# Two encoder layers on one core: the last layer's products over 512 tokens in one matmul, and a layer norm applied when products leave PSUM

## The chip, the cores and the metric

The kernel runs on one core of a Trainium2 chip. The metric is the device time of one launch in microseconds; the lower, the better. Times of the kernel before are from three runs; the profile is of one further execution.

## The reference

Two layers work on 512 tokens of width 1024, float32, with 16 learned meta tokens put ahead of them (528 columns in all, the meta tokens dropped at the end). In each layer one normalised input feeds one wide projection, four mixers run on parts of it, each mixer's result is projected and gated, and an MLP follows:

```python
def hybrid_layer(h, ...):
    hn = rmsnorm(h, norm_g[0])
    (gate_pre, cb, cc, cv, mq, mk, mv, mo, mi, mf, su, cq, ckv, kr) = split_cols(hn @ w_in)
    gates = jax.nn.sigmoid(gate_pre).reshape(bsz, L, N_BRANCH, D)
    ys = (short_conv_mixer(...), mlstm_mixer(...), s5_mixer(...), mla_mixer(...))
    ...
        term = gates[:, :, bi] * (ys[bi] @ w_branch[start:start + w])
    ...
    h = h + rmsnorm(merged @ w_out, norm_g[1])
    hn = rmsnorm(h, norm_g[2])
    ff = jnp.square(jax.nn.relu(hn @ w1)) @ w2
    return h + rmsnorm(ff, norm_g[3])
```

`rmsnorm` divides a token's row by the root of its mean square and multiplies by a gain per channel. Since the division is one number per token, it can be made before a product or after it.

## The kernel before, in words

Activations lie channel by channel: 128 channels on the partitions, tokens along the free axis. A product takes a weight tile of 128 x 128 as the stationary operand and streams tokens. Every float32 operand is split in a high and a low part, and a term of a product is three matmuls into one PSUM bank (`triple`, lines 473 to 477): high weight by high activation, high by low, low by high. `prod` (line 465) runs over the terms, eight for a product over 1024 channels.

The tokens stand in two halves (`HALF`, line 24): 272 columns with the meta tokens and 256. In the last layer the meta tokens are only needed as keys and values, so most products there run over `LAST` (line 25), two halves of 256. Each weight tile is therefore used for two separate accumulations of 256 columns.

Weights come from HBM in units of 512 KB; ScalarE makes the high part (`cut`), VectorE the low part (`rest`). Activations lie in 32 slots of SBUF. `Wide` keeps 528 columns of two channel tiles in one slot; `Tok` keeps a half of the tokens, four channel tiles to a slot, so that the two halves of one channel tile lie in different slots.

The order of the work is written by a planner inside the program. It follows the main line of products and keeps an estimate of the time on TensorE, VectorE and ScalarE (class `Model` and the engine wrappers). Side work (the mixers, norms, evictions) is a set of generators; `tick` gives each a turn when its operands are due and VectorE and ScalarE are at most 2.05 us ahead of TensorE by these estimates (line 501). `drain` puts TensorE off until a generator has ended, `room` until slots are free. So a change of one piece moves all that comes after it.

A layer begins with its 17 units of the input projection (`unit`, line 1567). Its operand is the layer input times the gain, not yet divided by the norm, since the norm is not known so early; `evac` (line 1516) multiplies by the norm row `R` when a product leaves PSUM. Meanwhile `rescale` (line 1615) reads the layer input a second time from HBM, scales it with gain and norm and splits it anew into `X2`; `fresh` (line 1638) puts each half in place of the first copy as soon as it is there. From then on a product leaves PSUM by a plain ScalarE copy, and a gate by ScalarE's tanh straight from PSUM (`gate`, line 1675). mLSTM waits until the state-space branch S5 and the rescaling have ended (line 1662). The branches follow (`branch`, line 1689), the attention inputs, the output projection, and the MLP in two rounds of 16 units up (`up`, `relu2`) and 16 down (`down`, line 1994). `place` reserves slots for weight tiles that must be held over both halves.

## Time and profile before

| what | value |
|---|---|
| median of three runs | 1978.32 us |
| the three runs | 1979.14, 1974.87, 1978.32 us |
| the profiled execution's own time | 1978.66 us |
| its span, first to last instruction | 1976.8 us |
| mean granted TensorE clock | 0.984 |

The span is what the profile's shares refer to; 1.9 us of the execution lie around it. A row of TensorE is a matmul, named by where it writes, what streams and what is stationary (`mm<-H,hi` streams a slot against the high part of a weight). Durations of matmuls overlap, so the pace is read from starts. The clock column is the granted clock as a share of full speed.

### The profile page before, as it was taken

What the parts mean: (1) busy time and instruction counts of PE and PEld (TensorE: products, weight loads), DVE (VectorE), ACT (ScalarE), POOL (GpSimd) and SP (SyncE); (2) the same over time, 40 slices, a digit from 0 to 9 for tenths busy, and PEclk for the clock granted to TensorE, in tenths of its full rate; (3) what the DMA queues carried; (4) which work ended last, traced back from release to release, by engine and by line L of the source; (5) the groups of instructions that cost most, each with busy time, mean ns of one, the idle gap of its engine ahead of it and who ended that gap; (6) DMA issues with size and microseconds to landing.
All of it is one profiled execution on the core that took longest, in us unless ns stands there. A gap on an engine that the chain in (4) does not pass through costs nothing.

```text
span 1976.8 us, 36671 instructions
## 1 busy us (share of the span) xinstructions
PE 1911.3 (97%) x15111; PEld 1843.4 (93%) x15111; DVE 1124.9 (57%) x2785; ACT 810.6 (41%) x1752; POOL 30.2 (2%) x64
## 2 busy tenths in 40 slices
PE   7999899999989999999999999999999999999999
PEld 6998887889989999999999998899899999999998
DVE  6977675654466774244366765666545666214534
ACT  4245543543434652244233444435344455224421
POOL 0000000100000000000000000001000000000000
PEclk9999899999989999999999999999999999999999
DMA  4332121312223233222234322133212522232231
GB/s 144 102 110 81 43 65 51 95 56 63 65 94 111 86 128 118 77 95 86 90 104 179 103 86 65 38 100 116 61 47 66 171 65 86 84 99 86 89 105 65
DMA packets 56072, 176.65 MB, mean 89 GB/s; under 512 B 6433, under 2 KB 13857, under 8 KB 55905
## 3 DMA queue, kind: packets, MB, share of 16 engines
q1 hardware_dynamic: 55904, 174.31, 27.3%
q8 instruction: 118, 1.93, 0.4%
q14 instruction: 50, 0.40, 0.1%
HBM read 165.24 MB, written 7.96 MB: 88 GB/s over the span
## 4 chain that ended last, share of the span: by engine, by line
PE 84%; DVE 8%; ACT 5%; issue 2%; DMA 1%; SPq 0%; DVEq 0%; ACTq 0%
PE mm L189 68%; PE ac L189 8%; PE mx L189 6%; DVE H L162 4%; ACT H L162 3%; PE mx L195 2%; DMA raw<-in_wall 1%; DVE tq L162 1%; DVE lo L162 1%; ACT wk L162 1%; ACT hi L162 0%; DVE acc L162 0%; DMA H<-in_wall 0%; DVE a_mx L162 0%; ACT tq L162 0%
## 5 line engine op out<-in xcount | busy, mean ns | idle before, releaser
L189 PE MATMUL mm<-H,hi 128*128 128x256 f32 (+1 forms) x7104 | 1337.2, 289 | 21.0 <-ACT hi L162 7.9
L189 PEld LDWEIGHTS mm<-H,hi 128*128 128x128 f32 x7104 | 1118.7, 192 | 34.1 <-ACT hi L162 7.9
L189 PE MATMUL mm<-H,lo 128*128 128x256 f32 (+1 forms) x3552 | 1015.7, 286 | 6.5 <-DVE lo L162 6.5
L189 PEld LDWEIGHTS mm<-H,lo 128*128 128x128 f32 x3552 | 681.6, 192 | 7.5 <-DVE lo L162 7.5
L162 DVE TENSOR_TENSOR lo<-raw,hi 128x1024 fp32r<-128x1024 f32 (+1 forms) x246 | 296.1, 1214 | 176.3 <-ACT hi L162 173.2
L162 ACT ACTIVATE hi<-raw 128x1024 fp32r<-128x1024 f32 (+1 forms) x246 | 253.8, 1046 | 108.3 <-PE mm L189 64.4
L189 PE MATMUL mm<-H,H 128*128 128x256 f32 (+1 forms) x1608 | 200.2, 285 | 2.4 <-DVE H L162 2.1
L189 PEld LDWEIGHTS mm<-H,H 128*128 128x128 f32 x1608 | 196.6, 190 | 3.7 <-DVE H L162 3.7
L189 PE MATMUL ac<-H,hi 128*128 128x256 f32 (+1 forms) x752 | 145.0, 289 | 4.2 <-DVE H L162 4.0
L162 ACT ACTIVATE gt<-mm 128x256 f32<-128x256 f32 (+1 forms) x185 | 71.4, 386 | 189.0 <-PE mm L189 181.1
L162 ACT ACTIVATE H<-mm 128x256 f32<-128x256 f32 (+5 forms) x152 | 60.1, 400 | 177.7 <-PE mm L189 175.3
L189 PEld LDWEIGHTS ac<-H,hi 128*128 128x128 f32 x752 | 118.1, 190 | 6.5 <-DVE H L162 5.9
L189 PE MATMUL mx<-H,H 128*128 128x132 f32 (+10 forms) x496 | 108.9, 357 | 11.2 <-ACT H L162 6.9
L162 DVE TENSOR_TENSOR gt<-gt 128x256 f32<-128x256 f32 (+1 forms) x110 | 47.0, 428 | 113.2 <-ACT H L162 113.1
L189 PE MATMUL ac<-H,lo 128*128 128x256 f32 (+1 forms) x376 | 106.7, 284 | 0.0
L189 PEld LDWEIGHTS mx<-H,H 128*128 128x128 f32 (+1 forms) x496 | 71.0, 192 | 30.0 <-issue 15.2
L162 ACT ACTIVATE tq<-H 128x256 f32<-128x256 f32 (+2 forms) x105 | 39.3, 407 | 115.5 <-DVE H L162 115.5
L162 DVE TENSOR_REDUCE a_mx<-mx 128x1 f32<-128x144 f32 (+5 forms) x80 | 33.3, 436 | 76.5 <-PE mx L189 75.5
L162 DVE TENSOR_TENSOR acc<-acc,tq 128x256 f32<-128x256 f32 (+1 forms) x123 | 52.6, 427 | 37.1 <-ACT tq L162 34.2
L162 ACT ACTIVATE wk<-mx,a_mx 128x512 f32<-128x512 f32 (+4 forms) x88 | 40.0, 462 | 79.6 <-DVE a_mx L162 79.6
L189 PEld LDWEIGHTS ac<-H,lo 128*128 128x128 f32 x376 | 71.5, 190 | 0.0
L162 DVE TENSOR_TENSOR H<-H,tq 128x256 f32<-128x256 f32 (+2 forms) x154 | 65.3, 424 | 4.6 <-ACT H L162 1.3
(243 smaller groups left out, 1507.2 us busy)
## 6 DMA issues: line engine op xcount, KB each, us to landing
raw<-in_wall SPq DMA_DIRECT2D x274, 512.0 KB
raw<-in_wuq SPq DMA_DIRECT2D x6, 384.0 KB
H<-in_xT SPq DMA_DIRECT2D x4, 528.0 KB
hspill<-H SPq DMA_DIRECT2D x4, 528.0 KB
H<-hspill SPq DMA_DIRECT2D x4, 528.0 KB
H<-in_wall SPq DMA_DIRECT2D x4, 512.0 KB
mats<-H SPq DMA_DIRECT2D x4, 512.0 KB
H<-mats SPq DMA_DIRECT2D x4, 512.0 KB
```

What stands on the lines that cost most here:

```text
L162: i = f(*a, **k)
L189: i = self.eng.matmul(out, lhsT=lhsT, rhs=rhs, start=start, stop=stop)
L195: i = self.eng.transpose(out, in_, identity)
```

## The change

In the last layer the two halves of most products become one product of 512 columns, a whole PSUM bank. For this the slots are allocated in pairs, one tile of SBUF for two slots: `sides` gives the slots so that the halves of a channel tile lie at the same place in the two slots of a pair, and `Tok.at` then returns one operand of two runs of 256 columns. Pairs are kept apart by the kind of data (`kinds`), so free slots are counted by `avail`. The products' evictions are cut back into halves (`cut_up`), but for the MLP's, which take 512 columns at once (`ups`).

`rescale`, `X2` and `fresh` are gone. The first, undivided copy serves for the whole layer, in both layers, and gates and attention inputs are multiplied by `R` on VectorE when they leave PSUM. mLSTM waits only for free slots. `prod` gives side work a turn after every second term of a wide product, and the last layer holds one weight tile less ahead in its first MLP round and none in its last.

```diff
-LAG2 = 7
+LAG2 = 6
...
+    def whole(n=1):
+
+        ps = [i // 2 for i in free if i % 2 == 0 and i + 1 in free]
+        ps.sort(key=lambda p: max(free.index(2 * p), free.index(2 * p + 1)))
+        return ps[:n]
+
+    def beside(kind):
+        return [i for i in free if i ^ 1 not in free and kinds[i // 2] == kind]
+
+    def avail(kind="f"):
+
+        return 2 * len(whole(NSLOT)) + len(beside(kind))
...
+    def sides():
+
+        p, q = whole(2)
+        return [2 * p, 2 * q, 2 * p + 1, 2 * q + 1]
...
         def at(self, m, c0, c1):
+            if c0 < CUT < c1:
+                o, p = m % 4 * CUT + c0, self.hs[m // 4].pair
+                return p.rearrange("p (a n) -> p a n", n=SLOT)[:, :, o:o + CUT - c0]
             i = c0 // CUT
-            return self.t[2 * i + m // 4][:, m % 4, c0 - HALF[i][0]:c1 - HALF[i][0]]
+            o = 0 if i == 0 else META if self.ids else 0
+            return self.t[2 * i + m // 4][:, m % 4, c0 - HALF[i][0] + o:c1 - HALF[i][0] + o]
...
             if i % 4 == 3:
                 ahead(deep[0])
+            if i % 4 == 3 or i % 2 and ps.shape[1] > CUT:
                 tick()
...
-        X2 = Tok(0), Tok(0)
-        scaled_ = []
-
-        def rescale():
-            for c, (c0, c1) in enumerate(HALF):
-                hs = []
-                while not s5_on or len(free) < 4:
-                    yield "w"
-                for x in X2:
-                    x.more()
-                for m in range(11):
-                    if m < 8:
-                        hs.append(wk_t()[:, :c1 - c0])
-                        dma(hs[-1], (hspill if l else xT)[:, m, c0:c1])
-                    if 1 < m < 10:
-                        t = hs[m - 2]
-                        while PE.t < model.due(t):
-                            yield "w"
-                        stt(t, t, gain(l, 0, m - 2), R[:, c0:c1], ALU.mult, ALU.mult)
-                        copy(r(X2[0].at(m - 2, c0, c1)), t)
-                    if m > 2:
-                        tt(r(X2[1].at(m - 3, c0, c1)), hs[m - 3], X2[0].at(m - 3, c0, c1), ALU.subtract)
-                        yield 0
-                yield
-                scaled_.append(c)
-
-        def fresh():
-
-            for c in scaled_[len(swapped):]:
-                for x, x2 in zip((XH, XL), X2):
-                    x.drop(c)
-                    x.hs[2 * c:2 * c + 2], x.t[2 * c:2 * c + 2] = x2.hs[2 * c:2 * c + 2], x2.t[2 * c:2 * c + 2]
-                swapped.append(c)
...
-                fresh()
                 unit(w, first[j], c)
...
-                e_ml = spawn(mlstm(l, last, made["qk"], made["v"], made["o"], ym, lambda: e_s5 not in gens and e_rs not in gens))
+                e_ml = spawn(mlstm(l, last, made["qk"], made["v"], made["o"], ym, lambda: True))
...
+        WIDE = ((META, T),) if last else HALF
+
+        def cut_up(c0, c1):
+
+            return [(i, max(a, c0) - c0, min(b, c1) - c0) for i, (a, b) in enumerate(QH) if a < c1 and b > c0]
+
         def gate(w, dst_of):
-            for i, (c0, c1) in enumerate(QH):
+            for c0, c1 in WIDE:
                 ps = bank()[:, :c1 - c0]
-                fresh()
                 prod(ps, terms(w, 0, 8, xh, xl, c0, c1))
-                g = dst_of(i)
-                if i in swapped:
-                    act(g, ps, AF.Tanh, scale=0.5)
-                else:
-                    tt(g, ps, R[:, c0:c1], ALU.mult)
+                for i, a, b in cut_up(c0, c1):
+                    g = dst_of(i)
+                    tt(g, ps[:, a:b], R[:, QH[i][0]:QH[i][1]], ALU.mult)
                     act(g, g, AF.Tanh, scale=0.5)
                 lent[0] = 0
                 tick()
...
-                for i, (c0, c1) in enumerate(QH):
+                for c0, c1 in WIDE:
                     ps = bank()[:, :c1 - c0]
                     prod(ps, terms(w, (m % per) * nk * 128, nk, hi, lo, c0, c1))
-                    d = mg.at(m, c0, c1)
-                    if b == 0:
-                        stt(d, gt[i], 1.0, ps, ALU.add, ALU.mult)
-                    else:
-                        t = tq()[:, :c1 - c0]
-                        stt(t, gt[i], 1.0, ps, ALU.add, ALU.mult)
-                        tt(d, d, t, ALU.add)
+                    for i, a, e in cut_up(c0, c1):
+                        d = mg.at(m, *QH[i])
+                        if b == 0:
+                            stt(d, gt[i], 1.0, ps[:, a:e], ALU.add, ALU.mult)
+                        else:
+                            t = tq()[:, :e - a]
+                            stt(t, gt[i], 1.0, ps[:, a:e], ALU.add, ALU.mult)
+                            tt(d, d, t, ALU.add)
...
-        drain(e_rs)
-        fresh()
...
-        for i, halves in ((3, HALF), (4, HALF), (0, QH), (1, QH), (2, QH)):
+        for i, cols in ((3, HALF), (4, HALF), (0, WIDE), (1, WIDE), (2, WIDE)):
             w = W(l, U_IN + 17 + i)
-            for c0, c1 in halves:
+            for c0, c1 in cols:
                 ps = bank()[:, :c1 - c0]
-                fresh()
                 prod(ps, terms(w, 0, 8, xh, xl, c0, c1))
-                copy(rawq.at(i, c0, c1) if i < 3 else rawk.at(i - 3, c0, c1), ps)
+                for j, (h0, h1) in enumerate(HALF if i > 2 else QH):
+                    a, e = max(h0, c0), min(h1, c1)
+                    if a < e:
+                        d = rawq.at(i, a, e) if i < 3 else rawk.at(i - 3, a, e)
+                        tt(d, ps[:, a - c0:e - c0], R[:, a:e], ALU.mult)
...
+        def ups(m, w):
+            if not last:
+                for c in range(2):
+                    up(m, c, w)
+                return
+            ps = mm_t()
+            prod(ps, terms(w, 0, 8, xh, xl, META, T))
+            hh, hl = hid[m % 16 // 8]
+            t = wk_t()[:, :T - META]
+            t3 = t.rearrange("p (a n) -> p a n", a=2)
+            act(t, ps, AF.Relu)
+            hi = hh.at(m % 8, META, T)
+            act(r(hi), t3, AF.Square)
+            tt(t, t, t, ALU.mult)
+            tt(r(hl.at(m % 8, META, T)), t3, hi, ALU.subtract)
...
-        def down(d, m, c, w, first=True, fin=True, ps=None):
-            c0, c1 = QH[c]
-            n = c1 - c0
-            ps = ps if ps is not None else mm_t()[:, :n]
+        def down(d, m, cs_, w):
+
+            c0, c1 = QH[cs_[0]][0], QH[cs_[-1]][1]
+            ps = mm_t()[:, :c1 - c0]
...
+        ALL = [(0, 1)] if last else [(0,), (1,)]
...
-        lagh = place([(l, U_W2 + 16 + u) for u in range(12, 16)])
+        lagh = [] if last else place([(l, U_W2 + 16 + u) for u in range(12, 16)])
```

The order of the instructions moves with it, in three places.

TensorE, last layer, first MLP round, where one weight tile's turn ends and the next begins. Before (a bank `mm` holds 256 columns; the same weight `_19324` then comes a second time for the other half):

```order
L189 MATMUL mm_19539<-H5_18222,hi_19324 128x256
L189 MATMUL mm_19539<-H19_18224,hi_19324 128x256
L189 MATMUL mm_19539<-H5_18222,lo_19325 128x256
L189 MATMUL mm_19575<-H13_18524,hi_19324 128x256
L189 MATMUL mm_19575<-H23_18526,hi_19324 128x256
L189 MATMUL mm_19575<-H13_18524,lo_19325 128x256
```

Now:

```order
L192 MATMUL mm_17561<-H8_16441,H6_17056 128x512
L192 MATMUL mm_17561<-H15_16439,H6_17056 128x512
L192 MATMUL mx_17597<-ones_94,acc_17506 128x1 x2
L192 MATMUL mm_17621<-H0_16438,hi_17496 128x512
L192 MATMUL mm_17621<-H4_16440,hi_17496 128x512
L192 MATMUL mm_17621<-H0_16438,lo_17497 128x512
```

Each weight tile now has one accumulation of 512 columns, and the next bank begins with the next weight tile.

TensorE, layer 0: mLSTM's first transposes (`m_lf`), with S5's matmuls of 132 columns and gate products around them. Before, they stand between gate products, behind all of S5:

```order
L189 MATMUL mm_2687<-H27_1849,hi_2429 128x256
L189 MATMUL mm_2687<-H9_1851,hi_2429 128x256
L189 MATMUL mm_2687<-H27_1849,lo_2430 128x256
L195 MATMUL mx_2718<-cs_92,m_lf_2216 4x16
L195 MATMUL mx_2718<-cs_92,m_lf_2216 4x128 x2
L195 MATMUL mx_2723<-cs_92,m_lf_2216 4x128 x2
L189 MATMUL mm_2741<-H18_985,hi_2556 128x272
```

Now:

```order
L192 MATMUL mx_2060<-H15_958,H2_960 128x132
L192 MATMUL mx_2060<-H8_961,H2_960 128x132 x2
L198 MATMUL mx_2077<-cs_92,m_lf_1765 4x16
L198 MATMUL mx_2077<-cs_92,m_lf_1765 4x128 x2
L198 MATMUL mx_2082<-cs_92,m_lf_1765 4x128 x2
L192 MATMUL mx_2089<-H15_958,H2_960 128x132
```

They have moved into the output products of S5's first group, ahead of its whole second group.

VectorE, layer 0, a gate and its branch product (`tq`, then the sum in a slot) beside attention's softmax steps. Before:

```order
L162 TENSOR_SCALAR H_4243<-wk,a_sm 128x16
L162 TENSOR_SCALAR wk<-wk,a_sm 128x256
L162 TENSOR_TENSOR lo<-raw,hi 128x1024
L162 SCALAR_TENSOR_TENSOR tq<-gt,mm 128x272
L162 TENSOR_TENSOR H_1865<-H_1865,tq 128x272
L162 SCALAR_TENSOR_TENSOR tq<-gt,mm 128x256
L162 TENSOR_TENSOR H_1865<-H_1865,tq 128x256
L162 TENSOR_REDUCE a_mx<-mx 128x1 x2
```

Now:

```order
L162 TENSOR_SCALAR H_354<-wk,a_sm 128x16
L162 TENSOR_SCALAR wk<-wk,a_sm 128x256
L162 TENSOR_TENSOR gt<-mm,R 128x272
L162 TENSOR_TENSOR gt<-mm,R 128x256
L162 SCALAR_TENSOR_TENSOR tq<-gt,mm 128x272
L162 TENSOR_TENSOR H_189<-H_189,tq 128x272
L162 SCALAR_TENSOR_TENSOR tq<-gt,mm 128x256
L162 TENSOR_TENSOR H_189<-H_189,tq 128x256
L162 TENSOR_TENSOR lo<-raw,hi 128x1024
L162 TENSOR_REDUCE a_mx<-mx 128x1 x2
```

Each gate now adds two multiplications by `R` on VectorE, ahead of its branch product.

## Rows read from the trace of the kernel before

**Rows 1.** The page: span, busy times (us, share, instructions), granted clock in 40 slices.

```profile
span 1976.8 us, 36671 instructions
...
PE 1911.3 (97%) x15111; PEld 1843.4 (93%) x15111; DVE 1124.9 (57%) x2785; ACT 810.6 (41%) x1752; POOL 30.2 (2%) x64
...
PEclk9999899999989999999999999999999999999999
```

**Rows 2.** The page: the chain that ended last, shares of the span by engine.

```profile
PE 84%; DVE 8%; ACT 5%; issue 2%; DMA 1%; SPq 0%; DVEq 0%; ACTq 0%
```

**Rows 3.** Busy time by stretches, instructions behind each engine; columns in the first line.

```profile
core 0: us, PE busy (x) PEld busy (x) DVE busy (x) ACT busy (x) POOL busy (x), PEclk, DMA share, GB/s
140.00:240.00 100.00, 88.81 (x675) 86.20 (x675) 69.74 (x170) 56.00 (x124) 1.78 (x9) 0.93 0.23 72
200.00:220.00 20.00, 16.35 (x112) 16.34 (x112) 16.73 (x38) 9.11 (x21) 0.00 (x0) 0.83 0.18 54
540.00:560.00 20.00, 15.21 (x101) 11.74 (x100) 8.59 (x33) 8.71 (x29) 0.00 (x0) 0.77 0.00 0
1120.00:1140.00 20.00, 18.04 (x137) 17.88 (x137) 14.61 (x38) 8.52 (x19) 0.00 (x0) 0.91 0.39 124
1140.00:1160.00 20.00, 16.57 (x141) 16.17 (x139) 9.86 (x24) 11.89 (x26) 0.00 (x0) 0.96 0.09 27
1160.00:1180.00 20.00, 19.63 (x146) 19.63 (x147) 16.83 (x51) 6.39 (x13) 1.14 (x4) 0.87 0.42 129
1800.00:1900.00 100.00, 100.00 (x842) 100.00 (x841) 47.90 (x79) 40.34 (x75) 0.00 (x0) 1.00 0.29 90
```

**Rows 4.** Order of time on TensorE, last layer's MLP: start us, duration us, operation.

```profile
1710.04 0.40 PE L189 MATMUL mm<-H,hi 128*128 128x256 f32 x2
...
1715.76 0.40 PE L189 MATMUL mm<-H,hi 128*128 128x256 f32 x2
```

**Rows 5.** The same for the last layer's value projection, 512 columns.

```profile
1350.22 0.40 PE L189 MATMUL mm<-lo,H 128*128 128x512 f32 x1
...
1355.08 0.40 PE L189 MATMUL mm<-lo,H 128*128 128x512 f32 x1
```

**Rows 6.** VectorE by form: out<-in, shapes, count, busy us, mean ns, idle before.

```profile
L162 DVE TENSOR_TENSOR lo<-raw,hi 128x1024 fp32r<-128x1024 f32 x240 | 290.4, 1221 | 164.2 <-ACT hi L162 161.1
...
L162 DVE TENSOR_TENSOR gt<-gt 128x256 f32<-128x256 f32 x83 | 35.2, 424 | 97.9 <-ACT H L162 97.8
...
L162 DVE TENSOR_TENSOR H<-wk,H 128x256 fp32r<-128x256 f32 x29 | 12.2, 422 | 16.0 <-ACT H L162 15.7
...
L162 DVE TENSOR_TENSOR H<-mm,R 128x256 f32<-128x256 f32 x21 | 8.8, 420 | 10.1 <-PE mm L189 8.5 <-ACT R L162 1.7
...
L162 DVE SCALAR_TENSOR_TENSOR wk<-wk,pr,R 128x272 f32<-128x272 f32 x16 | 7.9, 495 | 0.4 <-DMA wk<-hspill 0.4
...
L162 DVE TENSOR_TENSOR H<-ac,H 128x512 fp32r<-128x512 f32 x8 | 5.5, 691 | 16.7 <-ACT H L162 16.7
```

**Rows 7.** ScalarE by form, the first copy of a weight tile.

```profile
L162 ACT ACTIVATE hi<-raw 128x1024 fp32r<-128x1024 f32 x240 | 248.7, 1052 | 108.3 <-PE mm L189 64.4 <-DMA raw<-in_wall 42.2 <-PE mx L189 1.5
```

**Rows 8.** Order of time on TensorE, three waits: in brackets idle us and releaser.

```profile
203.66 2.18 PE L189 MATMUL mx<-H,H 128*128 128x132 f32 x8 [3.65 <-ACT H L162]
...
359.43 0.44 PE L195 MATMUL mx<-cs,tq 128*128 128x128 f32 x2 [2.44 <-DVE tq L162]
...
1160.37 0.58 PE L189 MATMUL mm<-H,lo 128*128 128x256 f32 x1 [3.80 <-DVE lo L162]
```

**Rows 9.** Order of time before 1160 us: a VectorE row, then ScalarE.

```profile
1158.14 0.71 DVE L162 TENSOR_TENSOR H<-H,H 128x528 fp32r<-128x528 f32 x1 [3.73 <-ACT H L162]
...
1150.08 3.31 ACT L162 ACTIVATE H<-mx 32x132 f32<-32x132 f32 x8 [2.34 <-PE mx L189]
1153.42 0.43 ACT L162 ACTIVATE H<-wk 128x272 fp32r<-128x272 f32 x1
1153.87 3.25 ACT L162 ACTIVATE H<-mx 32x132 f32<-32x132 f32 x8
```

More of the change, by code (lines that the diff above doesn't have):

```diff
@@ L186, in matmul @@
         n = max(128, math.prod(rhs.shape[1:]))
+        if len(rhs.shape) == 3:
+            out = out.rearrange("p (a n) -> p a n", a=rhs.shape[1])
         cost = self.price(4 * n if rhs.dtype == F32 else n, lhsT.shape[0])
-        self.model.issue(self, cost, out, (lhsT, rhs), 0.21, start)
+        parts = [rhs] if len(rhs.shape) < 3 else [rhs[:, j] for j in range(rhs.shape[1])]
+        self.model.issue(self, cost, out, (lhsT, *parts), 0.21, start)
         i = self.eng.matmul(out, lhsT=lhsT, rhs=rhs, start=start, stop=stop)
@@ L296, in trunk, with __init__, more @@
     class Wide:
-        def __init__(self, n=8):
-            self.hs, self.t = [], []
-            for _ in range(-(-n // 2)):
+        def __init__(self, n=8, kind="f"):
+            self.hs, self.t, self.kind = [], [], kind
+            k = -(-n // 2)
+            for _ in range(k // 2):
+                for s in two(kind):
+                    self.more(s)
+            if k % 2:
                 self.more()
-        def more(self):
-            self.hs.append(Slot())
+        def more(self, slot=None):
+            self.hs.append(slot or Slot(self.kind))
             self.t.append(self.hs[-1].v(0, 2, T))
@@ L524, in tick, with room @@
                 return
-    def room(n):
+    def room(n, kind="f"):
         spins = 0
-        while len(free) < n:
+        while avail(kind) < n:
             spins += 1
@@ L808, in mlstm @@
         yield
-        while not ready() or len(free) < 5:
+        while not ready() or avail() < 5:
             yield "w"
@@ L870, in tail @@
             nqt, nq, qi0 = max(1, n // 128), min(128, n), TS.index(q0)
-            while len(free) < 1:
+            while avail() < 1:
                 yield "w"
@@ L1153, in s5_ahead @@
     def s5_ahead(l):
-        while len(free) < 4:
+        while avail() < 4:
             yield "w"
@@ L1176, in s5_group @@
         p0 = gp * 4
-        while len(free) < (5 if gp else 6):
+        while avail() < (5 if gp else 6):
             yield "w"
@@ L1258, in s5 @@
             yield from s5_params()
-        while len(free) < 10:
+        while avail() < 10:
             yield "w"
@@ L1276, in s5 @@
         release(hu, *ht)
-        while len(free) < 2:
+        while avail("r") < 2:
             yield "w"
-        y5[0] = Wide(2), Wide(2)
+        y5[0] = Wide(2, "r"), Wide(2, "r")
         for m in range(2):
@@ L1288, in lora_norm @@
     def lora_norm(l, raw, nk, box, gcol, inv, halves, ready):
-        while not ready() or len(free) < nk:
+        while not ready() or avail("r") < nk:
             yield "w"
-        box.append(Wide(2 * nk))
+        box.append(Wide(2 * nk, "r"))
         y = box[0]
@@ L1417, in mla_attn @@
             if st is not None:
-                while heads() <= st[0] or (len(yq[0]) <= st[0] // 2 and len(free) < 2):
+                while heads() <= st[0] or (len(yq[0]) <= st[0] // 2 and avail("r") < 2):
                     yield "w"
@@ L1920, in up @@
             (evac or relu2)(m, c, ps)
+            tick()
+        def ups(m, w):
+            if not last:
+                for c in range(2):
[11 more added lines that the diff above has]
+            tt(r(hl.at(m % 8, META, T)), t3, hi, ALU.subtract)
             tick()
@@ L2004, in down @@
                 tt(a, ps, a, ALU.add)
-                if last and c and m == 7:
-                    act(accs[2], a, AF.Square)
-                else:
-                    sumsq(accs[c], a, m == 0)
+                for c in cs_:
+                    a = FF.at(m, *QH[c])
+                    if last and c and m == 7:
+                        act(accs[2], a, AF.Square)
+                    else:
+                        sumsq(accs[c], a, m == 0)
             tick()
+        ALL = [(0, 1)] if last else [(0,), (1,)]
         for m in range(8):
@@ L2027, in trunk @@
             ws.append([W(l, U_W2 + 16 + m * 2 + kg) for kg in range(2)])
-            down(1, m, 0, ws[m])
-            if m < 6:
-                down(1, m, 1, ws[m])
+            for cs_ in ALL if m < 6 else [(0,)]:
+                down(1, m, cs_, ws[m])
         for hh in hid:
@@ L2062, in trunk @@
                 slack[0] = SLACK0
-            down(1, m, 1, ws[m])
+            down(1, m, (1,), ws[m])
         for hh in hid:
```

108 lines of the change are left out of this document (61 added, 47 removed).

## The prediction, made before the changed kernel ran

> **What bounds the kernel now.** I read the page first. TensorE is busy for 97% of the span, VectorE for 57%, ScalarE for 41%, and the granted clock is at full speed in nearly every slice [rows 1]. The chain that ended last says the same: 84% of it is TensorE, 8% VectorE [rows 2]. So the kernel is bound by the rate of matmuls, and the 65.5 us in which TensorE is not busy (1976.8 - 1911.3) are its waits. The second view is the busy time by stretches [rows 3]. From 1800 to 1900 us, inside the last layer's MLP, TensorE never stops: 842 matmuls of 256 columns in 100 us, 118.8 ns each. From 140 to 240 us, where layer 0 runs its state-space branch beside the gates, it is busy for 88.8 us, its clock averages 0.93, and VectorE has 69.7 us of work. So the change must be judged twice: what it does to the pace where TensorE runs without a stop, and what it does to the waits at the head of each layer.
>
> The third view is the order of time on TensorE, for the pace itself. In the last layer's MLP a triple of three 256-column matmuls starts every 0.3575 us: 16 triples from 1710.04 to 1715.76, 119.2 ns a matmul [rows 4]. The kernel already has one place with 512 columns of the same operand type, the value half of the key/value projection: seven triples from 1350.22 to 1355.08, 231.4 ns a matmul [rows 5]. These two groups price the main part of the change.
>
> **The change part by part.**
>
> *Merged products.* In the order of the changed program 2454 matmuls of 512 columns (1456 + 728 + 148 + 74 + 48, by operand and bank) stand where 4908 of 256 stood. All are in the last layer: gates, branch products, the query path, the gated output of the state-space branch, 26 of 32 MLP rows up, 14 of 16 down. Two matmuls of 256 take 237.6 ns by rows 3 or 238.4 ns by rows 4; one of 512 takes 231.4 ns. The difference is 6.2 to 7.0 ns, and I take 6.5: 2454 x 6.5 ns = 16.0 us. It lies on the path, since TensorE is the bound there. The other end is 0, if the paired operand (two runs of 256 in two slots) streams more slowly than the contiguous 512 of rows 5, so that one matmul takes what two took; no row shows a paired read. I stay by rows 5: same type, same bank width, only the address pattern differs. That the saving is so small, 3% of a pair, is the point to see: columns are not saved, only the fixed part of one matmul. A line through 119.0 ns at 256 and 231.4 at 512 has a fixed part of 6.6 ns and 0.439 ns a column.
>
> The Trainium skill, "TensorE: Matmul & The Clock Gate", section "Back-to-back issue gap", gives N / 2.4 + 2.5 ns a matmul at full clock: 109.2 and 215.8 ns, so a gain of 2.5 ns a pair and 6.1 us in all, and the sum below would come to 1971.5 us instead of 1961.7. Both of its paces lie under what rows 4 and 5 show, so the trace does not agree with it here.
>
> *Second normalised copy gone.* Before, each layer reads its input again in 16 DMAs, scales it (16 VectorE operations, 0.495 us at 272 columns [rows 6]), copies it on ScalarE and subtracts (16 on VectorE, 0.422 us at 256 [rows 6]), and later products leave PSUM without the norm. Over two layers VectorE loses 32 scalings and, by the changed order, 33 such subtractions: 32 x 0.495 + 33 x 0.422 = 29.8 us, at the crowded heads. The 32 DMAs leave SP's queue, where weight loads stood behind them. I cost both at nothing on the path: the VectorE work mostly ran beside a busy TensorE.
>
> *Norm at evacuation instead.* In the changed order 128 more products are multiplied by the norm row on VectorE (76 gates, 52 others), at 0.420 us [rows 6] and, for the 36 of 272 columns, a little more: 54 us. Merged MLP rows give back 7.4 us of VectorE (102 operations of 0.424 us become 52 of 0.691 us [rows 6]), merged down rows some 1.6 us. Net VectorE: 54 - 29.8 - 7.4 - 1.6 = +15 us on 1124.9. What hides it is TensorE: a gate and its branch product take 30 x 231.4 ns = 6.9 us in the last layer, and VectorE's share of them is two norms, two fused products, two adds and 1.25 weight residuals, 6 x 0.42 + 1.25 x 1.22 = 4.0 us [rows 6]. Cost on the path: 0, and some 3 us if attention, which shares these engines, ends later; it ends exposed in layer 0 already, 4.8 us not busy from 540 to 560 us [rows 3].
>
> *mLSTM starts earlier.* Its wait for the state-space branch and for the second copy is dropped (now only free slots hold it). On TensorE its transposes now stand inside the state-space branch's first group of layer 0, where they stood after its second. So both share VectorE and ScalarE at the head. Three waits are concerned. At 203.66 us TensorE waited 3.65 us for the branch's tables [rows 8], behind a VectorE that was scaling the second copy. At 1160.37 it waited 3.80 us for a weight residual: VectorE had sat 3.73 us on a subtraction whose copies stood on ScalarE behind two runs of eight small evictions, 3.31 and 3.25 us, and two copies of 0.43 us of the rescaling [rows 8, 9]. Only these 0.86 us are gone. At 359.43 it waited 2.44 us at the end of mLSTM [rows 8], which now ends far sooner. I credit these with -4 us and charge the new crowd +3: net -1. Bounds: all three and the clock behind them gone, -16 us; or the heads' losses doubled, +18 to +29 (both below).
>
> *Slots in pairs, one weight tile less held ahead in the last MLP, more turns for side work.* They add no instruction. Dropping the last reserved weight slots could expose a weight load: with 5.7 us of matmuls (48 x 119 ns) ahead of it and 1.05 + 1.22 us of copy and residual a tile, two tiles [rows 6, 7], it is covered. Cost 0.
>
> The sum is made against the profiled execution's 1978.66 us, 0.34 us over the median of 1978.32: 1978.66 - 16.0 - 1 = 1961.7, say **1962 us**.
>
> **The rivals.**
>
> *A smaller gain a pair* (chance 0.12). No row shows a paired read. If the second run of the pair costs half of a matmul's fixed part again, 3.3 ns of 6.6, a pair gains 3.2 ns: 2454 x 3.2 = 7.9 us, and 1978.66 - 7.9 - 1 = 1969.8 us. If it costs all of it, the change does not do what it says, and the time is 1978.66 - 1 = 1977.7 us (chance 0.08). For both: only the contiguous read of rows 5 is measured. Against: rows 4 and 5 lie on one line with the operand's length, and a new address run has no price of its own there. The section of the Trainium skill named above, with its 2.5 ns a pair, would come to much the same as the first of the two, 1971.5 us.
>
> *Slower: the crowded head* (chance 0.10). mLSTM and the state-space branch run at once on VectorE, which already has 69.7 us of work in the 100 us from 140 to 240 [rows 3]. TensorE loses there 11.2 us not busy and 7 us of clock (100 x 0.07), 18 us. If these losses double in layer 0 alone, the time is 1962 + 18 = 1980 us. If those of layer 1's head double as well (1120 to 1180 us: 2.0 + 3.4 + 0.4 not busy, 1.8 + 0.8 + 2.6 of clock [rows 3]), 11 more make 1991 us, slower than before. It decides from 16 us of added waits on. Against it: the program's planner gives side work a turn only while VectorE and ScalarE are within 2.05 us of TensorE by its own prices, and 14.9 us a layer of rescaling leave the same place.
>
> *The heads clear* (chance 0.15): with the rescaling gone, the three waits [rows 8] vanish, 9.9 us, and with them the clock lost behind two of them, 20 x 0.17 + 20 x 0.13 = 6.0 us in the stretches from 200 and from 1160 us [rows 3]. Then 1978.66 - 16.0 - 15.9 = 1946.8 us. For it: VectorE scaled the second copy right ahead of the first wait. Against it: the state-space branch's own chain of copies stays.
>
> **How the numbers follow.** The forecast has 0.55. A difference under 0.2% (4 us) can't be told from no change. Faster: 0.55 + 0.15 + most of the 0.12, with a little taken off for the forecast's own spread, 0.80. Within 0.2%: the no-gain case and the mild end of the crowded head, 0.11. Slower: 0.09. The range reaches from the cleared heads, 1947, to the crowded head in layer 0, 1980, and leaves out the head crowded in both layers and anything better than cleared.
>
> **What would show each step.** Merged products: triples of 512 columns in the last MLP every 0.69 us; 0.71 us means no gain. The stretch from the last MLP's start to the end should lose some 8 us (1296 of the 2454 pairs lie there). Norm at evacuation: VectorE at 1125 + 15 us with no new TensorE wait in the gates. Head: TensorE's waits from 140 to 260 and from 1120 to 1180 us no larger than before. The prediction is wrong if the 512-column triples are not faster than two of 256, or if the heads give back over 10 us.

## The result, and the profile after

| | before | after |
|---|---|---|
| median of 4 runs, us | 1976.59 (1974.11 to 1979.14) | 1947.24 (1942.79 to 1949.72) |
| ratio, 95% interval | | 0.9849 [0.9823, 0.9875] |
| profiled execution, us | 1978.66 | 1949.72 |

The kernel became 29 us faster, 1.5%; the forecast was 16 us, 0.8%. The page of the changed kernel, with the chain's line by engine:

```profile
span 1947.7 us, 31665 instructions
...
PE 1886.0 (97%) x12657; PEld 1711.7 (88%) x12657; DVE 1136.8 (58%) x2788; ACT 783.4 (40%) x1633; POOL 30.1 (2%) x64
...
PEclk9999999999999999999999999999999999999999
...
PE 87%; DVE 6%; ACT 4%; issue 1%; DMA 1%; SPq 0%; DVEq 0%; ACTq 0%
```

Against [rows 1, 2] the bound is the same: TensorE at 97%. It is busy 25.3 us less (1911.3 - 1886.0) and idle 3.8 us less (65.5 to 61.7), and VectorE has 11.9 us more. The stretches that answer to [rows 3]:

```profile
core 0: us, PE busy (x) PEld busy (x) DVE busy (x) ACT busy (x) POOL busy (x), PEclk, DMA share, GB/s
140.00:240.00 100.00, 86.96 (x641) 82.89 (x640) 68.27 (x180) 48.01 (x111) 1.69 (x7) 0.93 0.18 57
200.00:220.00 20.00, 17.95 (x124) 17.05 (x124) 15.27 (x41) 7.67 (x22) 0.00 (x0) 0.91 0.09 27
540.00:560.00 20.00, 14.33 (x103) 12.28 (x104) 9.90 (x35) 7.99 (x25) 0.00 (x0) 0.91 0.08 27
1140.00:1160.00 20.00, 16.83 (x79) 13.73 (x78) 9.42 (x27) 11.97 (x25) 0.00 (x0) 0.91 0.17 54
1800.00:1900.00 100.00, 100.00 (x433) 81.09 (x432) 38.59 (x47) 31.07 (x44) 0.00 (x0) 1.00 0.30 100
```

In the last MLP 433 matmuls stand for 842. Their pace, in the order of time on TensorE (one row per triple is shown, the first and the last of 17; start us, duration us, operation):

```profile
1780.02 0.40 PE L192 MATMUL mm<-H,lo 128*128 128x512 f32 x1
...
1791.14 0.40 PE L192 MATMUL mm<-H,lo 128*128 128x512 f32 x1
```

16 triples in 11.12 us are 0.695 us a triple and 231.7 ns a matmul, as in the contiguous operand of [rows 5]. So the pairs are read as fast as foreseen. The heads did not clear: from 140 to 240 us TensorE is not busy for 13.0 us, and was not for 11.2 [rows 3]. In the same view, three waits of the changed kernel to set beside [rows 8] (idle us and releaser in brackets):

```profile
181.46 1.56 PE L198 MATMUL mx<-cs,H 128*128 128x128 f32 x6 [2.85 <-ACT H L162]
...
463.65 0.52 PE L192 MATMUL mm<-H,hi 128*128 128x272 f32 x2 [2.29 <-DVE gt L162]
...
1152.60 0.50 PE L192 MATMUL mm<-H,lo 128*128 128x512 f32 x1 [3.17 <-DVE lo L162]
```

The wait for a weight residual in layer 1 shrank from 3.80 to 3.17 us. The other two of [rows 8] are gone: S5's of 3.65 us (in e5 below, which only drops the second copy, it is gone already) and mLSTM's of 2.44 us. But others stand in their place. The 2.85 us at 181.46 come ahead of transpositions (`mx<-cs,H`); e6 and e1 below, which also have the early start and no second copy, wait 2.83 us ahead of the same ones, and e5 and e2, without the early start, do not. And a gate in layer 0 now waits 2.29 us for VectorE. So the 29 us are neither the forecast's sum nor the rival of the cleared heads, although that one named 1946.8 us.

**Two parts of a time.** Executions of one kernel differ by several us, in large part with the granted clock: the changed kernel's 1942.79 us had 0.993, its 1949.72 had 0.988. So each run is split in two: span x mean granted clock, "at full clock" below, and the rest, lost to the clock. Over 29 runs the kernel before has 1945.1 us at full clock, with a standard deviation of 1.3, and loses 30.2. The changed kernel has 1924.3 (4 runs) and loses 20.4. So by this split **20.8 us came at full clock and 9.8 us from the clock**. The split is a convention, and a rough one. Over all 163 executions on record, a clock higher by 0.001 went with a span shorter by some 1.3 us among executions of one kernel, where the split takes it for 1.95 us; at that rate the clock would account for some 6 of the 9.8 us. And the changed kernel's four executions differ at full clock by a standard deviation of 3.0 us, so that its 1924.3 is known to about 1.5 us.

### The profile page after: what moved, and what is told of

Same layout as the page of the kernel before. It is cut to its first block, busy times and chain, and to the rows that moved or that the text cites. A ratio compares the mean times of both kernels' runs of the same rounds, so it can differ in the third digit from the quotient of the medians.

```text
span 1947.7 us, 31665 instructions
## 1 busy us (share of the span) xinstructions
PE 1886.0 (97%) x12657; PEld 1711.7 (88%) x12657; DVE 1136.8 (58%) x2788; ACT 783.4 (40%) x1633; POOL 30.1 (2%) x64
## 4 chain that ended last, share of the span: by engine, by line
PE 87%; DVE 6%; ACT 4%; issue 1%; DMA 1%; SPq 0%; DVEq 0%; ACTq 0%
PE mm L192 70%; PE ac L192 9%; PE mx L192 6%; DVE H L162 3%; ACT H L162 3%; PE mx L198 2%; DVE tq L162 1%; DVE lo L162 1%; ACT wk L162 1%; DMA raw<-in_wall 1%; DVE acc L162 0%; ACT hi L162 0%; ACT tq L162 0%; DMA H<-in_wall 0%; DVE a_mx L162 0%
## 5 line engine op out<-in xcount | busy, mean ns | idle before, releaser
L192 PE MATMUL mm<-H,hi 128*128 128x256 f32 (+2 forms) x5792 | 1291.9, 318 | 21.1 <-ACT hi L162 7.1
L192 PEld LDWEIGHTS mm<-H,hi 128*128 128x128 f32 x5792 | 958.6, 191 | 92.5 <-DVE H L162 7.9
L192 PE MATMUL mm<-H,lo 128*128 128x256 f32 (+2 forms) x2896 | 911.4, 315 | 4.9 <-DVE lo L162 4.9
L192 PEld LDWEIGHTS mm<-H,lo 128*128 128x128 f32 x2896 | 554.5, 191 | 37.1 <-DVE lo L162 5.9
L192 PE MATMUL mm<-H,H 128*128 128x256 f32 (+2 forms) x1320 | 168.7, 288 | 1.1 <-DVE H L162 1.1
L192 PE MATMUL ac<-H,hi 128*128 128x256 f32 (+2 forms) x620 | 140.4, 317 | 3.6 <-DVE H L162 3.5
L162 ACT ACTIVATE H<-mm 128x272 f32<-128x272 f32 (+5 forms) x92 | 39.8, 436 | 159.9 <-PE mm L192 157.4
L192 PE MATMUL ac<-H,lo 128*128 128x256 f32 (+2 forms) x310 | 96.6, 311 | 1.1 <-DVE lo L162 1.1
L162 ACT ACTIVATE gt<-gt 128x272 f32<-128x272 f32 (+1 forms) x96 | 38.1, 421 | 133.0 <-DVE gt L162 124.5
L162 ACT ACTIVATE H<-H 32x264 f32<-32x264 f32 (+6 forms) x132 | 59.4, 475 | 70.8 <-DVE H L162 70.0
L162 DVE TENSOR_TENSOR H<-H,tq 128x256 f32<-128x256 f32 (+2 forms) x154 | 65.5, 425 | 7.5 <-ACT H L162 4.2
```

Source lines behind the costliest of these rows:

```text
L162: i = f(*a, **k)
L192: i = self.eng.matmul(out, lhsT=lhsT, rhs=rhs, start=start, stop=stop)
```

## The experiments

All of them are below, each measured against the kernel before on its own chip (medians of before there: 1975.5 to 1977.8 us); the last two columns are means over the runs.

| run | edit | median us | ratio [95%] | at full clock | lost to clock |
|---|---|---|---|---|---|
| | before | 1977.0 | | 1945.1 | 30.2 |
| e5 | before, norm at evacuation | 1978.3 | 1.0003 [0.9993, 1.0012] | 1952.2 | 24.5 |
| e4 | before, mLSTM early | 1972.2 | 0.9978 [0.9965, 0.9992] | 1942.1 | 29.0 |
| e6 | before, both | 1977.5 | 1.0001 [0.9989, 1.0013] | 1956.2 | 19.6 |
| e1 | after, nothing merged | 1967.4 | 0.9937 [0.9920, 0.9954] | 1942.5 | 22.1 |
| e8 | after, only the MLP merged | 1957.8 | 0.9899 [0.9884, 0.9913] | 1934.5 | 21.5 |
| e9 | after, only the mixers merged | 1952.0 | 0.9878 [0.9859, 0.9898] | 1932.7 | 18.0 |
| | after | 1947.2 | 0.9849 [0.9823, 0.9875] | 1924.3 | 20.4 |
| e2 | after, mLSTM waits | 1957.0 | 0.9890 [0.9874, 0.9907] | 1930.0 | 24.9 |
| e7 | before, rows (16, 272) | 1963.0 | 0.9922 [0.9904, 0.9939] | 1937.3 | 23.0 |
| e11 | before, rows (0, 272) | 1963.6 | 0.9931 [0.9914, 0.9948] | 1934.9 | 27.0 |
| e12 | before, rows (16, 256) | 1955.8 | 0.9886 [0.9868, 0.9904] | 1928.8 | 24.9 |
| e18 | before, rows (64, 256) | 1977.3 | 0.9999 [0.9990, 1.0009] | 1944.9 | 30.0 |
| e13 | e7, mLSTM early | 1958.3 | 0.9902 [0.9887, 0.9917] | 1934.5 | 22.0 |
| e10 | after, all rows (16, 272) | 1942.2 | 0.9821 [0.9806, 0.9836] | 1921.7 | 18.9 |
| e14 | after, places a | 1937.3 | 0.9806 [0.9791, 0.9821] | 1913.4 | 21.8 |
| e15 | after, places b | 1938.9 | 0.9821 [0.9804, 0.9839] | 1914.2 | 23.7 |
| e16 | after, all (64, 256) | 1945.8 | 0.9840 [0.9826, 0.9855] | 1921.9 | 21.9 |
| e17 | e16, nothing merged | 1968.8 | 0.9954 [0.9938, 0.9971] | 1947.6 | 19.2 |
| e19 | best places | **1933.1** | 0.9776 [0.9763, 0.9790] | 1912.0 | 18.9 |

"Rows (16, 272)" is the place of an operand in its slot: the first column it is read from, and the columns from one row to the next. The kernel before has its second halves at (0, 256).

### The heads: e5, e4, e6, e2

e5 takes the second copy away; e4 drops mLSTM's wait; e6 does both; e2 puts the wait back into the changed kernel.

```diff
-                e_rs = spawn(rescale())
-        drain(e_rs)
-        fresh()
-                copy(rawq.at(i, c0, c1) if i < 3 else rawk.at(i - 3, c0, c1), ps)
+                tt(rawq.at(i, c0, c1) if i < 3 else rawk.at(i - 3, c0, c1), ps, R[:, c0:c1], ALU.mult)
...
-mlstm(..., lambda: e_s5 not in gens and e_rs not in gens)
+mlstm(..., lambda: True)                      # e4, e6
+mlstm(..., lambda: e_s5 not in gens)          # e5; e2, where the changed kernel has True
```

e5: 

> The kernel before without the second normalised copy: rescale is not started, gates, units and the raw query and key rows take the norm on VectorE as they leave PSUM; mLSTM still waits for the state-space branch. Theory 1a (rescaling's removal gives the heads): 1965 us. Theory 1b (the early start gives them): 1977 us, and up to 1980 if the added products on VectorE make attention end later.

e4: 

> The kernel before with mLSTM's wait dropped (ready at once, only free slots hold it); rescaling and everything else stay. Theory 1a (rescaling's removal gives the heads): 1976.6 us, no change, or slower by the crowd at the heads (up to +10). Theory 1b (the early start gives them): 1965 us.

e6: 

> The kernel before with both head edits and nothing else: no second normalised copy (norm on VectorE at evacuation) and mLSTM not waiting for the state-space branch. Theory 1 (the two belong together: the second copy held the free slots that mLSTM waits for, so only without it does the early start reach layer 0): 1968 us, as the narrow version of the changed kernel, 9 us under before; mLSTM's wait of 2 to 5 us at its end in layer 0 is gone. Rival (the effects of the single edits add up, +1 and -5): 1973 us. If it stays over 1972 us, the paired slots, not these edits, gave the narrow version its gain.

e2: 

> The changed kernel with mLSTM's wait for the state-space branch put back (ready once e_s5 is done). Theory 1a (the 12 us that the merge does not explain come from the removed rescaling): no change, 1947 +- 3 us. Theory 1b (they come from mLSTM's early start): 1959 us. Between the two if both share.

Both theories on the heads fell: in the kernel before, the two edits together give nothing (1.0001). At full clock the norm at evacuation costs 7.1 us and the early start another 4.0, and a smaller loss to the clock (30.2 to 19.6) pays for both. Where the 7.1 go stands on TensorE: its waits for a gate tile (`gt`) of 0.3 us and more sum to 4.6 us before, for ScalarE, and to 12.3 us in e5, most of them for VectorE. The longest there are 2.33, 1.45 and 1.85 us in the last layer and 2.29 and 1.33 in layer 0. One of them in e1, which has it too, in the order of time over all engines:

```profile
1386.30 0.17 DVE L162 RECIPROCAL a_sm<-a_sm 128x2 f32<-128x2 f32 x1 [1.33 <-ACT wk L162]
...
1387.11 0.41 DVE L162 TENSOR_SCALAR wk<-wk,a_sm 128x384 f32<-128x384 f32 x1
1387.44 0.41 DVE L162 TENSOR_TENSOR gt<-mm,R 128x256 f32<-128x256 f32 x1
1387.77 0.41 DVE L162 SCALAR_TENSOR_TENSOR tq<-gt,mm 128x256 f32<-128x256 f32 x1
...
1387.91 0.50 PE L192 MATMUL mm<-H,hi 128*128 128x256 f32 x2 [2.33 <-DVE gt L162]
```

The multiplication by the norm stands in VectorE's queue behind a softmax, which itself waits 1.33 us for ScalarE and then scales four tiles. Only when this multiplication has read the bank is it free for the next gate. The product costs 0.41 us; the queue ahead of it costs 2.33.

In the changed kernel the early start does pay: without it (e2) the time is 9.8 us longer, 5.7 at full clock and 4.5 of clock. Its wait then stands at the end of mLSTM in layer 0, twice what it was before [rows 8]:

```profile
355.69 0.69 PE L198 MATMUL mx<-cs,tq 128*128 128x128 f32 x2 [5.20 <-DVE tq L162]
```

In e4, with the second copy in place, layer 0's waits are those of before (3.69 and 2.44 us), and nearly all of the gain comes in layer 1, between 1160 and 1346 us. In e6, without the copy, the wait of 2.44 us is gone. So the copy kept mLSTM back in layer 0; that it did so by its slots fits, but no run shows it.

### The merge: e1, e8, e9

```diff
-        WIDE = ((META, T),) if last else HALF
+        WIDE = QH if last else HALF            # e1, e8
...
-            if not last:
+            if True:                           # e1, e9: ups by halves
...
-        ALL = [(0, 1)] if last else [(0,), (1,)]
+        ALL = [(0,), (1,)]                     # e1, e9
```

e1: 

> The changed kernel with the last layer's products cut back to 256 columns (WIDE = QH, the MLP's rows and units by halves); paired slots, norm at evacuation and mLSTM's early start stay. Theory 1 (a 512-column matmul saves 6.8 ns against two of 256, 2454 pairs, 16.7 us, and the other 12 us of the gain are layer heads that the merge has nothing to do with): 1947.2 + 16.7 = 1964 us. Theory 2 (the merge also frees the last layer's heads): above 1968 us, to 1976 at most. Theory 3 (half of what the heads gave is the clock, which differs from run to run): 1964 us, but span times clock as in theory 1, and runs that differ by several us with their clock.

e8: 

> The changed kernel with only the last layer's MLP at 512 columns (1296 of 2454 pairs), its other products at 256. If a pair saves 4.9 ns once the rows lie alike (two of 118.3 ns against one of 231.7): 6.4 us under the narrow version, 1961 us. If it saves 6.5 ns as forecast: 8.4 us, 1959 us. If the merge's whole 20 us goes by pairs: 10.6 us, 1957 us.

e9: 

> The changed kernel with the last layer's MLP back at 256 columns, its gates, branches, query path at 512 (1158 pairs). Theory (the pace gives 1158 x 4.9 ns = 5.7 us, and merged gates free TensorE of three waits for gate tiles on VectorE, 5.7 us, and of the clock behind them, 2 us): 1954 us. Rival (only the pace counts): 1962 us.

At full clock the MLP's merge gives 8.0 us (e1 to e8), the mixers' 9.8 (e1 to e9), both together 18.2: they add up. Merged gates also have no wait like the one above: instead of the last layer's three gate waits for VectorE there is one of 1.28 us, for ScalarE. A bank of 512 columns takes 24 x 231.7 ns = 5.6 us to fill, and VectorE's 2.3 us would fit under that. So the mixers give 8.4 ns a pair and the MLP 6.2. But e1 without any merge is already 10 us faster than e6, which does the same arithmetic. What differs is the paired slots, with the lag and the order that go with them, and in e1 a triple of 256 columns takes 0.355 us, not 0.3575 [rows 4].

### The place of an operand: e7, e11, e12, e18, e13, e10

In the first four of these the instructions and their order are those of before; only the place of the second half's rows in their slots differs:

```diff
-                self.t.append(s.v(0, 4, c1 - c0))
+                self.t.append(s.v(0, 4, CUT))                                    # e11; e7 also adds META to the column
+                self.t.append(s.v(META * (len(self.hs) > 2), 4, c1 - c0))        # e12; e18: 4 * META
```

e7: 

> The kernel before with the second half's operand rows put 272 columns apart, from column 16 on, as the changed kernel's slots have them, instead of 256 apart; the same instructions in the same order. Theory (where the operand lies costs 1.7 ns a matmul: triples of 256 columns take 0.36 us in one half and 0.355 us in the other before, 0.355 us everywhere in the narrow version of the changed kernel): every 256-column triple at 0.355 us, TensorE's busy time 5 to 10 us lower, time 1967 to 1972 us. Rival (the pace comes from something else, the halves' weights or banks): no change, 1977 us.

e11: 

> The kernel before with the second half's rows 272 columns apart but from column 0 on. If the distance of 256 columns (1024 bytes) between rows costs the time: as with both, 1963 us and triples of 0.355 us. If the first column does: 1977 us and triples of 0.36 us.

e12: 

> The kernel before with the second half's rows still 256 columns apart but the first one from column 16 on. If the distance costs the time: 1977 us and triples of 0.36 us. If the first column does: 1963 us and triples of 0.355 us.

e18: 

> The kernel before with the second half's rows 256 apart from column 64 on; same instructions, same order. If column 64 is the best place for halves as for merged operands: at or under the run from column 16, 1950 to 1956 us, with layer 0's second halves at 113.3 ns. If the place acts otherwise on single halves: 1963 us or more.

This is the largest gain that the sum lacked. One edit of a place gives 14 us (e7, e11) or 22 (e12), another nothing (e18). Layer 0's MLP shows why. Below, one product of eight triples on TensorE, its first and last `lo` row, in the kernel before, e11, e12 (there also the product of the next weight tile) and e18:

```profile
832.94 0.28 PE L189 MATMUL mm<-H,lo 128*128 128x256 f32 x1
...
835.46 0.28 PE L189 MATMUL mm<-H,lo 128*128 128x256 f32 x1
```

```profile
831.73 0.28 PE L189 MATMUL mm<-H,lo 128*128 128x256 f32 x1
...
834.19 0.28 PE L189 MATMUL mm<-H,lo 128*128 128x256 f32 x1
```

```profile
835.47 0.28 PE L189 MATMUL mm<-H,lo 128*128 128x256 f32 x1
...
837.85 0.28 PE L189 MATMUL mm<-H,lo 128*128 128x256 f32 x1
...
841.22 0.28 PE L189 MATMUL mm<-H,lo 128*128 128x256 f32 x1
...
843.69 0.28 PE L189 MATMUL mm<-H,lo 128*128 128x256 f32 x1
```

```profile
832.36 0.28 PE L189 MATMUL mm<-H,lo 128*128 128x256 f32 x1
...
834.88 0.28 PE L189 MATMUL mm<-H,lo 128*128 128x256 f32 x1
```

Seven triples take 2.52, 2.46, 2.38 and 2.52 us: 120.0, 117.1, 113.3 and 120.0 ns a matmul, at (0, 256), (0, 272), (16, 256) and (64, 256). At (16, 272), e7, it is 118.1. At (16, 256) the next weight tile's product takes 117.8, from the same moving operand, and the two alternate; their mean is 115.5. In the last layer the same place gives no 113.3. There e12's two halves run alike, here 16 triples in 5.66 us, 117.9 ns a matmul:

```profile
1710.05 0.28 PE L189 MATMUL mm<-H,lo 128*128 128x256 f32 x1
...
1715.71 0.28 PE L189 MATMUL mm<-H,lo 128*128 128x256 f32 x1
```

So the place of the moving operand changes the pace, but first column and distance do not settle it alone. What else does was not tried: the slot itself, the place of the weight tile, which is loaded anew beside every matmul, and the PSUM bank are candidates. The first halves, 272 columns, stay at 126.1 ns in all of them. Neither "the distance costs" nor "the first column costs" holds: both change the pace, and not in one direction. TensorE's waits were left as they were: of 0.3 us and more, 58.35 us before and 57.31 in e7.

The clock moved too, and that stays open. e7 loses 7 us less to it than the kernel before, with the same waits. In layer 0, behind one of 3.65 us (before) and 3.79 us (e7), the stretches of before are

```profile
220.00:240.00 20.00, 17.25 (x119) 15.59 (x118) 9.74 (x23) 12.06 (x34) 1.25 (x8) 0.84 0.17 54
240.00:260.00 20.00, 20.00 (x137) 18.96 (x136) 11.88 (x43) 10.11 (x26) 0.00 (x0) 0.91 0.09 27
```

after 0.83 from 200 to 220 [rows 3], and those of e7

```profile
200.00:220.00 20.00, 17.45 (x132) 17.45 (x133) 16.98 (x36) 8.66 (x22) 0.00 (x0) 0.91 0.19 55
220.00:240.00 20.00, 16.99 (x132) 15.15 (x131) 10.66 (x26) 14.88 (x42) 1.24 (x8) 1.00 0.16 52
240.00:260.00 20.00, 20.00 (x157) 19.47 (x157) 14.04 (x47) 9.98 (x26) 0.00 (x0) 1.00 0.20 59
```

8.4 us lost against 1.8 (20 us times what is missing to 1.00), each a mean of stretches at 2.4 and at 1.2 GHz.

e13: 

> The kernel before with rows 272 apart from column 16 on and with mLSTM's wait dropped; the second normalised copy stays, nothing is merged. If the two edits add (7.8 and 3.0 us of the time at full clock, 1945.1 before): 1934.3 us at full clock, some 1957 us in all, 10 us under the narrow version of the changed kernel, which differs from it by the norm at evacuation; so that part would cost 8 us. If they do not add: 1963 us as with the rows alone.

e13 gives 1934.5 us at full clock, as the sum of the two edits, and 8.0 less than e1, from which it differs by the norm at evacuation, by the place of layer 0's hidden rows (2.6 us, e10 below), and by the lag and the order that go with the pairs. With these last two left aside, the norm costs 5 to 7 us where nothing is merged.

e10 puts the rows that the changed kernel still has at (0, 256), such as layer 0's hidden ones, to (16, 272):

```diff
-            c0, c1 = HALF[0 if self.ids else i]
+            c0, c1 = HALF[0]
...
-            o = 0 if i == 0 else META if self.ids else 0
+            o = META * i
```

e10: 

> The changed kernel with the operand rows 272 columns apart and from column 16 on also where it still has them 256 apart (the second half of layer 0's hidden rows and of both layers' other token tiles without sides); same instructions, same order. Theory (the place of a row costs 1.8 ns a 256-column matmul): 1 to 3 us less than the changed kernel, 1944 to 1946 us, and layer 0's MLP, 467.4 us long, about 2 us shorter. Rival (the 7.8 us came from one operand only): no change, 1947 us.

It gave 5 us, 2.6 at full clock, which the spread of the changed kernel's own runs leaves open by some 1.5. In the traces layer 0's MLP, from its first wait to the wait behind it, went from 460.8 to 458.8 us, the 2 us that the theory of the place asks for.

### The place of a merged operand: e14, e15, e16, e17, e19

In the last MLP no half needs the meta columns, so its rows can be 256 apart and begin at any column up to 64. `s` is that column; layer 0's tiles are no longer paired, and their second halves lie at (16, 256), in e16 and e17 at (64, 256).

```diff
+                self.t.append(s.v(self.s, 4, CUT - META) if self.s is not None else s.v(META if i and not self.ids else 0, 4, c1 - c0))
...
+                o = m % 4 * CUT + c0 if self.s is None else self.s + m % 4 * (CUT - META)
...
+        MH = Tok(2, sides() if last else None, s=16 if last else None)
```

e14: 

> The changed kernel with layer 0's token tiles unpaired, their second halves 256 apart from column 16 on, and the last layer's MLP operands 256 apart: its input from column 16, the first hidden rows from column 0, the second from column 32. If the place sets the pace of a 512-column matmul too: paces from about 226 to 240 ns that differ between the MLP's stages, 231.7 in none or one of them. If two runs of 256 in one operand cost the same anywhere: 231.7 ns in all three. Layer 0's MLP: 454 us from its first wait to its last, as with these rows in the kernel before, against 461 us in the changed kernel; so 1938 to 1942 us with the merged stages unchanged.

e15: 

> The same with the last layer's MLP input from column 64, the first hidden rows from column 8, the second from column 48. The same two expectations; if only the distance of rows matters, each stage has the pace that it had in the run with columns 16, 0 and 32.

e16: 

> The changed kernel with layer 0's second halves and the last layer's MLP operands 256 apart from column 64 on, still merged. If the place is what sets the pace: 226.7 ns in every merged stage of the MLP, 1296 x 5 ns = 6.5 us under the changed kernel there, and layer 0 as in the two runs before or better: 1934 to 1937 us.

e17: 

> The same places, nothing merged (last layer at 256 columns). If a merge saves something that no place gives: the last MLP's halves stay at 117 to 118 ns, so the run is 1296 x 8 to 10 ns = 10 to 13 us slower there than merged, 1955 us or more in all. If the place gives the same to halves: 113.3 ns, the last MLP as long as merged, and only the mixers' share is lost (1158 pairs at 4.9 ns and some 4 us of waits): 1945 to 1948 us.

e19: 

> The changed kernel with layer 0's second halves 256 apart from column 16 on and the last layer's MLP operands 256 apart from column 64 on. If the places add: the MLP at 226.7 ns a matmul throughout, 3 to 4 us under the run with columns 16, 0 and 32, layer 0 as there: 1933 to 1935 us, 13 us under the changed kernel. If they don't: 1937 us or more.

The paces, `lo` rows again: in e14 the input's products (from column 16, 8 triples), those of hidden rows 8 to 15 (from column 32, 7 triples) and 0 to 7 (from column 0, 6 triples):

```profile
1642.38 0.39 PE L192 MATMUL mm<-H,lo 128*128 128x512 f32 x1
...
1647.87 0.39 PE L192 MATMUL mm<-H,lo 128*128 128x512 f32 x1
...
1686.44 0.39 PE L192 MATMUL mm<-H,lo 128*128 128x512 f32 x1
...
1691.33 0.39 PE L192 MATMUL mm<-H,lo 128*128 128x512 f32 x1
...
1695.41 0.39 PE L192 MATMUL mm<-H,lo 128*128 128x512 f32 x1
```

228.8, 232.9 and (from 1691.33 on) 226.7 ns a matmul. In e15 the input from column 64, and hidden rows (0 to 7 from column 8, 8 to 15 from 48), 8 triples each:

```profile
1636.18 0.39 PE L192 MATMUL mm<-H,lo 128*128 128x512 f32 x1
...
1641.62 0.39 PE L192 MATMUL mm<-H,lo 128*128 128x512 f32 x1
...
1692.20 0.40 PE L192 MATMUL mm<-H,lo 128*128 128x512 f32 x1
...
1697.79 0.40 PE L192 MATMUL mm<-H,lo 128*128 128x512 f32 x1
```

226.7 and 232.9 ns. So a merged operand depends on its place as well, and differently: (64, 256), beside (0, 256), is its best place and the worst of single halves, which is why e16 missed its 1934 to 1937 us. e16 and e17 show it in one pair: with everything at (64, 256) the merge gives 25.7 us at full clock, 13.3 ns a pair in the MLP (2 x 120.0 - 226.7), against 4.9 at (16, 272) (2 x 118.3 - 231.7). Halves at 113.3 throughout would make the best merged pace worth nothing (2 x 113.3 = 226.6), but the last layer has shown none at that pace; against e12's 117.9 there, 226.7 still gives some 9 ns a pair. e19 takes the best place found for each, and beats both kernels: 1933.1 us, 43.7 under before and 14 under the changed kernel. It runs the merged products of the last MLP at 226.7 ns. Its page:

```profile
span 1930.7 us, 31665 instructions
...
PE 1865.2 (97%) x12657; PEld 1697.8 (88%) x12657; DVE 1135.6 (59%) x2788; ACT 783.3 (41%) x1633; POOL 30.2 (2%) x64
```

## Why the prediction was too small

The way and the bound were right, and the pace of a merged matmul was met to 0.3 ns (231.4 foreseen, 231.7 measured). The sum was 17 us; the spans differ by 30.6. Step by step, at full clock:

- **"Merged products", 16.0 us, at most 17.** Measured 18.2 (e1 to after). The pace gives 4.9 ns x 2454 = 12.0 us of it, not 16; most of the other 6 are gate waits that only the norm at evacuation had brought in. The step took 119.2 ns for a property of 256 columns, and part of it was the place of the second half.
- **"Slots in pairs ... They add no instruction ... Cost 0". This is the step that failed.** Pairing gives the second halves other rows, from (0, 256) to (16, 272). Such an edit alone gives 7.8 us at full clock and 13.7 in time (e7); from e6 to e1, with the other lag and the order that goes with the pairs, it is 13.7 us at full clock. About 5.5 us of that are fewer waits (67.8 to 62.3 us of those of 0.3 us and more), 4.5 of them for gate tiles. Of the other 8, the place accounts for some 5 (e7's 7.8 less the 2.6 of the rows that e1 still has at the old place); no run tells what the last 3 are. That an edit adds no instruction was taken to mean that it moves no time; where its operands lie was not asked.
- **"Norm at evacuation", 0, perhaps 3.** It costs 7.1 us where nothing is merged (e5). The count of VectorE's work per gate (4.0 of 6.9 us) was an average; attention's softmax stands ahead of the product in the queue. In the changed kernel the waits for gate tiles are down to 4.9 us, against 4.6 before, so there the 0 was nearly met. The norm at evacuation thus needs the merge of the gates; whether the merge needs it was not tried.
- **"mLSTM starts earlier", net -1, bounds -16 and +29.** In the changed kernel it is worth -5.7 us (e2), on the old slots +4.0 (e5 to e6).
- **The clock.** The sum has no term for it, only the rivals on the heads count it, and by the split it gave 9.8 us. The loss falls from 30.2 us to 24.5 when the second copy goes (e5), to 19.6 with the early start on top (e6; the early start alone leaves 29.0), and to 23.0 with the new places alone (e7). Why the place does it is not settled.

The steps follow one path of runs (before, e5, e6, e1, after), so they must add up: 7.1 + 4.0 - 13.7 - 18.2 = -20.8 us at full clock, and -9.8 of clock. Along it the place and the waits that went with the pairs, priced at nothing, are mostly cancelled by the norm and the early start, which cost more than foreseen. That the sum at full clock is off by only 4 us is therefore luck. The rest of the miss goes by the name of the clock, with the reserve made above. The rival of the cleared heads had the right number by luck too: two of its three waits are gone, but others came, and TensorE's waits of 0.3 us and more went only from 58.35 to 56.82 us.

The Trainium skill's N / 2.4 + 2.5 ns ("TensorE: Matmul & The Clock Gate", section "Back-to-back issue gap"), which that section gives for an isolated matmul and not for a stream with weight loads as here, makes 109.2 and 215.8 ns. No place reached it (113.3 and 226.7 at best), and its gain of 2.5 ns a pair was 4.9 at (16, 272) and 13.3 at (64, 256). The Trainium skill's "SBUF — State Buffer", section "Who interferes with whom", says that TensorE reads its two operands through ports of its own and waits for nobody. It says nothing of a price by the place; the rows above show one, without showing what TensorE meets there.

Left open: what sets the pace beside first column and distance (five places of single halves and seven of merged operands are no rule, and one of them has two paces), and why the clock loses less. Not tried: merged products with the second copy kept, and other places for the mixers' input, whose rows hold the meta columns.

## What to carry to other kernels

Where TensorE sets the end, the place of its moving operand in SBUF is a parameter of its own: try a few first columns and row distances with the same instructions, for each width apart, before a pace is taken for a property of the shape. When an edit moves buffers, price the move, even if it adds no instruction. And an operation that frees a PSUM bank costs what stands ahead of it in its engine's queue, not its own length.

## What the runs showed of the hardware that was not expected

A 256-column fp32r matmul took 113.3 to 120.0 ns and one of 512 columns 226.7 to 232.9 ns at full clock. With the instructions and their order unchanged, the place of the moving operand moved it within these bounds; at one place, (16, 256), it was 113.3 and 117.8 in turn, from one weight tile to the next. Two places, (0, 256) and (64, 256), were the worst for one width (120.0 ns) and the best for the other (226.7). And the mean granted clock differed between executions of one kernel, from 0.986 to 0.993, with times 6.8 us apart. Span times clock differed less between executions of a kernel (a standard deviation of 1.5 us, all kernels together) than the span did (2.1 us).
